# A weight load on another queue, thirteen split-weight buffers and merged small loads in a two-layer decoder

## The chip, the cores and the metric

The kernel runs on one core of one Trainium2 chip. The metric is the device time of one execution in microseconds (us). A core has five engines with queues of their own: TensorE (PE: matmuls; PEld is its weight load), VectorE (DVE), ScalarE (ACT), GpSimd (POOL) and SyncE (SP), which here only issues loads. A load (DMA) is issued from an engine's queue, runs on the core's DMA engines, and tells of its landing by a semaphore.

## The reference

Two decoder layers over 256 tokens of width 1024, in float32:

```python
for i in range(2):
    if i == 0:                                    # gated MLP over 128-position chunks
        u, v, q_mem = split(x @ a_w_in, [768, 1536])
        v = layer_norm(gelu(v), a_ln_v_g, a_ln_v_b)
        mix = gelu(u) * (tril(a_w_s) @ v + a_b_s)  # 12 groups of 64 columns
    else:                                         # causal attention, 12 heads of 64
        q, k, v, q_mem = split(x @ b_w_in, [768, 1536, 2304])
        mix = softmax(mask(q @ k.T / 8)) @ v
    mem_out = cross_attention(q_mem, mem @ w_mem_kv[i])   # 4 heads, 256 memory tokens
    x = layer_norm(ALPHA * x + concat(mix, mem_out) @ w_mix_out[i], ...)
    g, u = split(x @ w_ffn_in[i], 2)              # 2816 columns each
    x = layer_norm(ALPHA * x + (silu(g) * u) @ w_ffn_out[i], ...)
```

## The kernel before

**Split operands.** Matmuls run on float32r operands. To keep float32 accuracy each operand is split into a high part (`split`, L699: ScalarE casts it) and a low part (VectorE subtracts the high part from the original), and each product is three matmuls: high by high, low by high, high by low. So every weight passes through three stations: a load from memory into a `raw` tile, a cast on ScalarE, a subtract on VectorE, into an `spl` tile of which there are `HALF_BUFS` (12). An `spl` tile holds half a weight unit, usually 1024 columns in both parts. The feed-forward layers (`Ffn`, L1019) take their products by a scheme with seven products of sums of blocks (M1 to M7), so VectorE and some loads of GpSimd's queue also add raw weights.

**The planner.** The text of the kernel records every operation in `Plan` (L292), and `simulate` (L389) works out an order for each engine with costs written in the kernel (`Op.cost`, `Wire`). TensorE's operations keep the order of the text. For ScalarE, VectorE, GpSimd and SyncE the planner takes the operation that can start first, with a table `STAGES` (L296) of `(from, slip, idle, margin)` in ns, which says how far it delays a long operation for a short urgent one. Some copies may go to ScalarE or VectorE (`either`, L329), and the planner picks. `free["sync"], free["scalar"]` (L404) say from when on the two engines are taken as free. Then `emit` writes the instructions in that order; waits on semaphores are added for each data dependency. Loads of the SP and ACT queues signal eight completion semaphores (DMAHW0 to DMAHW7) that are given out in turn, in the order in which the instructions are laid out; a load that is given a semaphore which an earlier load still has to signal waits for that landing first.

**The start.** The first product, v = x @ a_w_in (`va` in the profile, L757 to L781), goes over eight row blocks of 128 weight rows. Row block k needs its 128 token rows of the transposed x (tile `x0raw`, here called X0 to X7) and its weight rows (`raw_v`, 768 columns, split into `spl_v`). Those of blocks 0 and 1 are loaded in two halves of 384 columns (192 KB), here W0a, W0b, W1a and W1b; later blocks in one load of 384 KB. For each block TensorE does six matmuls with the first half of the columns and then six with the second: W0a, W0b, W1a, W1b, and so on, in the order of the text. X0 is cast by VectorE, all other tokens and weights by ScalarE. X1 and X2 are issued from ScalarE's queue, behind two small copies (L742) that also make ScalarE load its activation table early; all else from SyncE's. Before all this, 28 matmuls on a constant (`warmup`, L746) keep TensorE busy.

**Small inputs.** The gain and bias of the gate's layer norm (`gv`, L1250) are two loads that repeat a row on 128 partitions; its spatial bias (`bsB`, L1270) six loads of 64 partitions; x for the residual (`xres`, L1329) two loads; the layer-norm gain and bias of layer 1 (`g1mix`, `b1mix`, L1462) two loads of 512 KB into tiles of their own.

Of the kernel before, what the change touches and what calls it, by code (L numbers as in the profile page):

```python
# [13 lines left out]
F32 = mybir.dt.float32  # L14
# [20 lines left out]
RAW_BUFS = 6  # L35
HALF_BUFS = 12
NFF = D_FF // 256
# [254 lines left out]
class Plan:  # L292


    ENGINES = ("tensor", "vector", "scalar", "gpsimd", "sync")
    STAGES = ((0, 300, 700, 300), (360000, 0, 700, 100), (405000, 300, 700, 300))  # L296

# [91 lines left out]
    def simulate(self, stages):  # L389
# [12 lines left out]
        free = {e: 0.0 for e in self.ENGINES}  # L402
        free["sync"], free["scalar"] = 800.0, 2100.0
        busy = dict(free)  # L404
# [280 lines left out]
def build(chip, tc, ins, out):  # L685
    ET = mybir.EngineType
    with (
# [30 lines left out]
        def bcast_row(row, n):  # L718
            return row.rearrange("(o n) -> o n", o=1).to_broadcast([P, n])
# [15 lines left out]
        def const_tile(shape, dtype, name):  # L735
            b = tile_of("const", shape, dtype, name, name)
            b.tile = const.tile(shape, dtype, name=name)
            return b

        mhalf = const_tile([P, 1], F32, "mhalf")  # L740
        chip.vector.memset(mhalf.tile, -0.5)
        for k in (1, 2):  # L742
            nc.scalar.copy(xraw[:, k, :1], mhalf)
        wt = ps.tile([P, 512], F32, tag="mm_3", name="warmup")
# [12 lines left out]
        for i in range(4):  # L757
            raw = raw_tile(f"raw_v{i}")
            for k in range(2):
                kk = 2 * i + k  # L760
                hl = tile_of("spl", [P, 2, 1024], F32R, "spl", f"spl_v{i}_{k}", HALF_BUFS)
                (nc.scalar if kk in (1, 2) else nc.sync).dma_start(xraw[:, kk, :], ins["xT"][kk * P:(kk + 1) * P, :])
                nh = 2 if kk < 2 else 1
                cuts = [(h * W_MIX // nh, (h + 1) * W_MIX // nh) for h in range(nh)]
                rk = raw[:, k * W_MIX:(k + 1) * W_MIX]
                for c0, c1 in cuts:
                    off = OFFS[f"v{i}"][0] + P * (k * W_MIX + c0)
                    nc.sync.dma_start(rk[:, c0:c1], ins["w"][off:off + P * (c1 - c0)].rearrange("(p n) -> p n", p=P))
                if kk == 0:
# [87 lines left out]
        def load_row(t, l, name):  # L857
            nc.sync.dma_start(t, bcast_row(ins[f"ln_{name}"][l, :], D))
            return t

        def load_gb(l, which):
            t = raw_tile(f"gb{l}{which}")
            return [load_row(t[:, i * D:i * D + D], l, f"{which}_{n}") for i, n in enumerate("gb")]


# [383 lines left out]
        gv = raw_tile("gv").rearrange("p (a c) -> p a c", a=2)[:, :, :W_MIX]  # L1249
        nc.sync.dma_start(gv[:, 0, :], bcast_row(ins["a_ln_v_g"][0, :], W_MIX))  # L1250
        nc.sync.dma_start(gv[:, 1, :], bcast_row(ins["a_ln_v_b"][0, :], W_MIX))
        mraws = []
# [16 lines left out]
        for i in range(3):  # L1269
            for j in range(2):  # L1270
                nc.sync.dma_start(bsB[i][j * HD:(j + 1) * HD], ins["bs"][j:j + 1, 2 * i:2 * i + 2, :].to_broadcast([HD, 2, P]))

# [55 lines left out]
        xres = [xr[:, tt, :] for tt in range(2)]  # L1328
        for tt in range(2):  # L1329
            nc.sync.dma_start(xres[tt], ins["x"][tt * P:(tt + 1) * P, :])  # L1330
        gb = load_gb(0, "mix")
# [129 lines left out]
        pts += mem_transposes(pr_mem, "1", (2, 3), acc_tile)  # L1461
        gb = [load_row(tile_of("act", [P, D], F32, t, n), 1, f"mix_{n[0]}") for t, n in (("g1", "g1mix"), ("b1", "b1mix"))]  # L1462
        op = OutProj(1, mix, "c")
# [37 lines left out]
def _pack(inp):  # L1501
# [27 lines left out]
    for i in range(6):  # L1529
# [9 lines left out]
        "wsT": np.ascontiguousarray(inp["a_w_s"][0].transpose(2, 0, 1)),  # L1539
        "bs": np.ascontiguousarray(inp["a_b_s"][0].reshape(6, 2, P).transpose(1, 0, 2)),  # L1540
        "a_ln_v_g": inp["a_ln_v_g"], "a_ln_v_b": inp["a_ln_v_b"],
        "ln_mix_g": inp["ln_mix_g"], "ln_mix_b": inp["ln_mix_b"],
# [21 lines left out]
```

## Time and profile before

| | |
|---|---|
| median of 3 runs | 550.85 us (550.62 to 551.06) |
| the profiled execution's own time | 550.73 us |
| its span, first to last instruction | 549.0 us |
| TensorE busy | 540.2 us (98%) |
| VectorE busy | 505.6 us (92%) |
| ScalarE busy | 358.7 us (65%) |
| loaded and stored | 132.48 MB, 241 GB/s over the span |
| granted TensorE clock, mean | 0.998 |

All times in the profile count from the start of the span. A row of the timeline gives start, length, engine, source line, operation, what it writes and reads, the number of merged instructions, and in brackets the idle time of the engine before it with what ended it. Almost all operations have the line L591, since the planner issues them there; tiles tell them apart. SPq, ACTq and POOLq are instructions that issue loads. Row blocks and halves are left out of the tiles' names: `raw_v` is W0a, W0b and so on, in the order of issue.

### The profile page before, as it was taken

What the parts mean: (1) busy time and instruction counts of PE and PEld (TensorE: products, weight loads), DVE (VectorE), ACT (ScalarE), POOL (GpSimd) and SP (SyncE); (2) the same over time, 40 slices, a digit from 0 to 9 for tenths busy, and PEclk for the clock granted to TensorE, in tenths of its full rate; (3) what the DMA queues carried; (4) which work ended last, traced back from release to release, by engine and by line L of the source; (5) the groups of instructions that cost most, each with busy time, mean ns of one, the idle gap of its engine ahead of it and who ended that gap; (6) DMA issues with size and microseconds to landing.
All of it is one profiled execution on the core that took longest, in us unless ns stands there. A gap on an engine that the chain in (4) does not pass through costs nothing.

```text
span 549.0 us, 7641 instructions
## 1 busy us (share of the span) xinstructions
PE 540.2 (98%) x2858; PEld 459.6 (84%) x2858; DVE 505.6 (92%) x687; ACT 358.7 (65%) x547; POOL 32.7 (6%) x42
## 2 busy tenths in 40 slices
PE   8999999999999999999999999999999999999994
PEld 7988878888888888888898888888888888888884
DVE  5799989999999999998997889889999999999985
ACT  6767845794849585776555689747756684947710
POOL 1110001000001000000000000100000000001001
PEclk9999999999999999999999999999999999999999
DMA  8999963767897979989667222772678979698902
GB/s 294 407 382 393 352 230 109 199 163 243 207 394 182 372 202 292 312 238 386 227 247 290 78 82 82 210 241 78 189 251 236 406 155 422 143 359 224 297 0 77
DMA packets 23637, 132.48 MB, mean 241 GB/s; under 512 B 2608, under 2 KB 6448, under 8 KB 9520
## 3 DMA queue, kind: packets, MB, share of 16 engines
q1 hardware_dynamic: 19856, 109.26, 50.9%
q0 software_dynamic: 3024, 22.02, 21.5%
q10 hardware_dynamic: 720, 0.72, 0.4%
q8 instruction: 22, 0.36, 0.3%
q14 instruction: 15, 0.12, 0.1%
HBM read 120.46 MB, written 1.05 MB: 221 GB/s over the span
## 4 chain that ended last, share of the span: by engine, by line
PE 98%; DMA 1%; DVE 1%; SPq 0%; ACT 0%; issue 0%; DVEq 0%
PE fog L591 11%; PE fof L591 11%; PE Xg L591 10%; PE Xf L591 10%; PE qk L591 6%; PE Zf L591 5%; PE Zg L591 5%; PE opc L591 4%; PE opa L591 4%; PE bv L591 3%; PE pu L591 3%; PE va L591 3%; PE pvm L591 3%; PE Yg L591 2%; PE Yf L591 2%; PE hkm L591 2%
## 5 line engine op out<-in xcount | busy, mean ns | idle before, releaser
L591 DVE TENSOR_TENSOR spl_s_M<-raw_s,spl_s_M 128x1024 fp32r<-128x1024 f32 x140 | 164.9, 1217 | 3.5 <-ACT spl_s_M L591 3.1
L591 ACT CAST spl_s_M<-raw_s 128x1024 fp32r<-128x1024 f32 x140 | 138.7, 1050 | 24.2 <-DMA raw_s<-in_w 19.1
L591 PE MATMUL fof<-spl_w,htf 128*128 128x512 f32 x264 | 63.9, 392 | 0.0
L591 PE MATMUL fog<-spl_w,htg 128*128 128x512 f32 (+1 forms) x282 | 63.9, 378 | 0.0
L591 PEld LDWEIGHTS fog<-spl_w,htg 128*128 128x128 f32 x282 | 50.2, 188 | 9.4
L591 PEld LDWEIGHTS fof<-spl_w,htf 128*128 128x128 f32 x264 | 49.0, 188 | 10.0
L591 DVE TENSOR_TENSOR spl_w<-raw_w,spl_w 128x1024 fp32r<-128x1024 f32 x44 | 53.4, 1216 | 0.0
L591 ACT CAST spl_w<-raw_w 128x1024 fp32r<-128x1024 f32 x44 | 45.6, 1050 | 10.3 <-DMA raw_w<-in_w 10.3
L591 DVE TENSOR_TENSOR raw_s<-raw_s,raw_s 128x2048 f32<-128x2048 f32 x19 | 43.4, 2284 | 0.1
L591 PE MATMUL qk<-x2T,spl_qk 128*128 128x512 f32 x192 | 34.8, 338 | 0.0
L591 PEld LDWEIGHTS qk<-x2T,spl_qk 128*128 128x128 f32 x192 | 29.3, 188 | 4.1
L591 PE MATMUL Zf<-spl_s_M,SfM 128*128 128x512 f32 x120 | 29.0, 390 | 0.0
L591 PE MATMUL Xg<-spl_s_M,SgM 128*128 128x512 f32 x120 | 29.0, 390 | 0.0
L591 PE MATMUL Zg<-spl_s_M,SgM 128*128 128x512 f32 x120 | 28.8, 389 | 0.0
L591 PE MATMUL Xf<-spl_s_M,SfM 128*128 128x512 f32 x120 | 28.8, 389 | 0.0
L591 PE MATMUL Xg<-spl_s_M,x3T 128*128 128x512 f32 x120 | 28.2, 389 | 0.0
L591 PE MATMUL Xf<-spl_s_M,x1T 128*128 128x512 f32 x120 | 28.2, 389 | 0.0
L591 PEld LDWEIGHTS Xg<-spl_s_M,x3T 128*128 128x128 f32 x120 | 22.5, 188 | 4.7
L591 PEld LDWEIGHTS Xf<-spl_s_M,x1T 128*128 128x128 f32 x120 | 22.5, 188 | 4.7
L591 PEld LDWEIGHTS Xf<-spl_s_M,SfM 128*128 128x128 f32 x120 | 22.5, 188 | 4.7
L591 PEld LDWEIGHTS Zg<-spl_s_M,SgM 128*128 128x128 f32 x120 | 22.5, 188 | 4.7
L591 PEld LDWEIGHTS Xg<-spl_s_M,SgM 128*128 128x128 f32 x120 | 22.4, 188 | 4.7
(253 smaller groups left out, 974.9 us busy)
## 6 DMA issues: line engine op xcount, KB each, us to landing
raw_s<-in_w SPq DMA_DIRECT2D x40, 1024.0 KB, 6.8
raw_w<-in_w SPq DMA_DIRECT2D x22, 1024.0 KB, 7.4
raw_s<-in_w POOLq DMA_DIRECT2D x11, 1024.0 KB, 8.5
raw_s<-raw_s POOLq DMA_DIRECT2D x10, 1024.0 KB, 7.6
raw_o<-in_w SPq DMA_DIRECT2D x8, 1024.0 KB, 7.0
raw_qk<-in_w SPq DMA_DIRECT2D x6, 1024.0 KB, 4.8
raw_u<-in_w SPq DMA_DIRECT2D x3, 1024.0 KB, 11.8
raw_bv<-in_w SPq DMA_DIRECT2D x4, 768.0 KB, 7.2
```

The costliest lines, as they stand in the source:

```text
L591: getattr(getattr(self.nc, c.engine), c.name)(*map(real, c.args), **{k: real(v) for k, v in c.kw.items()})
```

## The change

- `HALF_BUFS` goes from 12 to 13. The planner's `STAGES` get other limits at other points, and ScalarE counts as free 250 ns earlier.
- Start: the two small copies that stood ahead of ScalarE's loads go, and one copy of a constant (`one`) stands first on ScalarE. All tokens are issued from SyncE's queue. W0b is issued from ScalarE's queue, and its place in `raw_v` is filled with zeros by GpSimd first, so that the load waits for that fill.
- The gate's gain and bias are one input and one load of 768 KB; the spatial bias is repeated for 64 partitions on the host, and three loads of 128 partitions replace six; x is one load.
- The layer-norm gain and bias of layer 1 lose their own tiles. The class `Halves` loads each in two pieces of 512 columns: the gain into tiles that held the memory queries (`qm`), the bias into two of the nine `work` tiles (both go through `tile_of("act", ...)`).

```diff
-HALF_BUFS = 12
+HALF_BUFS = 13
...
-    STAGES = ((0, 300, 700, 300), (360000, 0, 700, 100), (405000, 300, 700, 300))
+    STAGES = ((0, 150, 700, 100), (135000, 0, 700, 100), (180000, 150, 700, 100))
...
-        free["sync"], free["scalar"] = 800.0, 2100.0
+        free["sync"], free["scalar"] = 800.0, 1850.0
...
+        one = const.tile([P, 1], F32, name="one")
+        chip.scalar.copy(one, chip.const_aps.tensor(1.0, [P, 1], F32))
         mhalf = const_tile([P, 1], F32, "mhalf")
         chip.vector.memset(mhalf.tile, -0.5)
-        for k in (1, 2):
-            nc.scalar.copy(xraw[:, k, :1], mhalf)
...
-                (nc.scalar if kk in (1, 2) else nc.sync).dma_start(xraw[:, kk, :], ins["xT"][kk * P:(kk + 1) * P, :])
+                nc.sync.dma_start(xraw[:, kk, :], ins["xT"][kk * P:(kk + 1) * P, :])
...
-                    nc.sync.dma_start(rk[:, c0:c1], ins["w"][off:off + P * (c1 - c0)].rearrange("(p n) -> p n", p=P))
+                    if kk == 0 and c0:
+                        nc.gpsimd.memset(rk[:, c0:c1], 0.0)
+                    (nc.scalar if kk == 0 and c0 else nc.sync).dma_start(rk[:, c0:c1], ins["w"][off:off + P * (c1 - c0)].rearrange("(p n) -> p n", p=P))
...
+        class Halves:
+
+            def __init__(self, n):
+                self.h = [tile_of("act", [P, 512], F32, f"qm{i}", f"g1mix{i}") if n == "g" else work_tile(f"b1mix{i}")
+                          for i in range(2)]
+                for h, (c0, c1) in zip(self.h, PIECES):
+                    nc.sync.dma_start(h, bcast_row(ins[f"ln_mix_{n}"][1, c0:c1], 512))
+
+            def __getitem__(self, key):
+                return self.h[key[1].start // 512]
...
-        nc.sync.dma_start(gv[:, 0, :], bcast_row(ins["a_ln_v_g"][0, :], W_MIX))
-        nc.sync.dma_start(gv[:, 1, :], bcast_row(ins["a_ln_v_b"][0, :], W_MIX))
+        nc.sync.dma_start(gv, ins["gv"].rearrange("(o a) c -> o a c", o=1).to_broadcast([P, 2, W_MIX]))
...
         for i in range(3):
-            for j in range(2):
-                nc.sync.dma_start(bsB[i][j * HD:(j + 1) * HD], ins["bs"][j:j + 1, 2 * i:2 * i + 2, :].to_broadcast([HD, 2, P]))
+            nc.sync.dma_start(bsB[i], ins["bs"][:, 2 * i:2 * i + 2, :])
...
-        for tt in range(2):
-            nc.sync.dma_start(xres[tt], ins["x"][tt * P:(tt + 1) * P, :])
+        nc.sync.dma_start(xr, ins["x"].rearrange("(a p) d -> p a d", p=P))
...
-        gb = [load_row(tile_of("act", [P, D], F32, t, n), 1, f"mix_{n[0]}") for t, n in (("g1", "g1mix"), ("b1", "b1mix"))]
+        gb = [Halves(n) for n in "gb"]
```

TensorE's instructions stand in the same order in both kernels. What moves at the start stands in two queues. ScalarE's first instructions before (`raw_v0` and `spl_v0_0` are the tiles of W0a and W0b, `spl_v0_1` that of W1a and W1b, `x0raw` the tokens; in brackets the semaphores that an instruction waits for, named by the engine or load that signals them):

```order
L591 ACT_TABLE_LOAD
L591 COPY x0raw_115<-mhalf_75 128x1 [waits DVE_49]
L591 COPY x0raw_115<-mhalf_75 128x1
L591 DMA x0raw_115<-in_xT 128x256 [waits Activation_49] x2
L591 CAST spl_v0_0_131<-raw_v0_113 128x384 [waits DMAHW0_49]
L591 CAST spl_v0_0_131<-raw_v0_113 128x384 [waits DMAHW2_49]
L591 CAST spl_v0_1_149<-raw_v0_113 128x384 [waits DMAHW3_49]
L591 CAST x0T_135<-x0raw_115 128x256 [waits DMAHW4_49]
```

And now:

```order
L741 ACT_TABLE_LOAD
L741 COPY one_75<-const-float32-1.0 128x1
L591 DMA raw_v0_114<-in_w 128x384 [waits DMAHW3_49,Pool_49]
L591 CAST spl_v0_0_131<-raw_v0_114 128x384 [waits DMAHW0_49]
L591 CAST spl_v0_1_141<-raw_v0_114 128x384 [waits DMAHW2_49]
L591 CAST spl_v0_0_131<-raw_v0_114 128x384 [waits DMAHW3_49]
L591 CAST x0T_134<-x0raw_118 128x256
```

Two loads of tokens, which waited for ScalarE's own copies, have become one load, W0b, which waits for GpSimd's fill and for DMAHW3. The cast of W1a now stands ahead of that of W0b.

SyncE's first loads before, W0a, X0, then W0b, W1a and W1b, then those of block 2 and on:

```order
L591 DMA raw_v0_113<-in_w 128x384
L591 DMA x0raw_115<-in_xT 128x256
L591 DMA raw_v0_113<-in_w 128x384 x3
L591 DMA raw_v1_127<-in_w 128x768
L591 DMA raw_v1_127<-in_w 128x768 [waits DMAHW0_49]
L591 DMA x0raw_115<-in_xT 128x256 [waits DMAHW1_49]
```

And now W0a, X0, W1a, X1, W1b, and on:

```order
L591 DMA raw_v0_114<-in_w 128x384
L591 DMA x0raw_118<-in_xT 128x256
L591 DMA raw_v0_114<-in_w 128x384
L591 DMA x0raw_118<-in_xT 128x256
L591 DMA raw_v0_114<-in_w 128x384
L591 DMA raw_v1_127<-in_w 128x768
L591 DMA x0raw_118<-in_xT 128x256
L591 DMA raw_v1_127<-in_w 128x768
L591 DMA x0raw_118<-in_xT 128x256 [waits DMAHW0_49]
L591 DMA raw_v2_137<-in_w 128x768 [waits DMAHW1_49]
L591 DMA x0raw_118<-in_xT 128x256 [waits DMAHW2_49]
L591 DMA raw_v2_137<-in_w 128x768 [waits DMAHW4_49]
```

X1 and X2 have moved in between the weight loads, and W1a has moved up into W0b's place. The ninth, tenth and eleventh load wait for semaphores 0, 1 and 2, the twelfth for 4.

More of the change, by code (lines that the diff above doesn't have):

```diff
@@ L1539, in _pack @@
         "wsT": np.ascontiguousarray(inp["a_w_s"][0].transpose(2, 0, 1)),
-        "bs": np.ascontiguousarray(inp["a_b_s"][0].reshape(6, 2, P).transpose(1, 0, 2)),
-        "a_ln_v_g": inp["a_ln_v_g"], "a_ln_v_b": inp["a_ln_v_b"],
+        "bs": np.repeat(inp["a_b_s"][0].reshape(6, 2, P).transpose(1, 0, 2), HD, axis=0),
+        "gv": np.concatenate([inp["a_ln_v_g"], inp["a_ln_v_b"]]),
         "ln_mix_g": inp["ln_mix_g"], "ln_mix_b": inp["ln_mix_b"],
```

## The prediction

> **What bounds the kernel now.** I read the page first: TensorE is busy for 98% of the span, and the chain that ended last runs 98% on it.
>
> ```profile
> PE 540.2 (98%) x2858; PEld 459.6 (84%) x2858; DVE 505.6 (92%) x687; ACT 358.7 (65%) x547; POOL 32.7 (6%) x42
> PE 98%; DMA 1%; DVE 1%; SPq 0%; ACT 0%; issue 0%; DVEq 0%
> ```
>
> So only a stretch in which TensorE stands still can be won or lost. The waits of TensorE (whom it waited for, us in total, times, longest) name two, and but for the very first instruction there are no others:
>
> ```profile
> PE va L591 <- ACT spl_v L591: 0.8, 1, 0.8
> PE va L591 <- DVE x0T L591: 0.2, 1, 0.2
> ```
>
> Both lie in the first 7 us. The chain in order of time (start, length, what) shows the longer of them, and what follows it:
>
> ```profile
> 1.72 4.33 DMA raw_v<-in_w
> ...
> 6.07 0.52 ACT spl_v L591
> ...
> 6.63 16.01 PE va L591 x90
> ```
>
> W0b, the second half of the first weight rows, is issued at 1.72 and lands at 6.05 (1.72 + 4.33); ScalarE casts it, and TensorE goes on at 6.63. From landing to matmul that is 0.58. In windows (length, TensorE's busy time, clock, DMA share, GB/s) the stretch behind those va matmuls is full to its end at 542.12:
>
> ```profile
> 4.00:6.63 2.63, 1.55 (x6) 1.00 1.01 344
> 22.64:542.12 519.48, 519.47 (x2735) 1.00 0.73 239
> ```
>
> The profiled execution took 550.73 us with a span of 549.0, so 1.7 lies around the span; the median of the runs is 550.85. I sum against 550.73. A measurement of this kernel tells about 0.2% (1.1 us) from no change.
>
> **The start, which sets the time.** The timeline before (start, length, engine, instruction, idle time before it):
>
> ```profile
> 0.84 3.15 PE L746 MATMUL warmup<-const-bfloat16-1.0 128*128 128x128 bf16 x28 [0.84 <-PEq L1553]
> 1.33 0.41 POOL L591 MEMSET mask<- 128x384 f32 x1
> 1.72 2.32 SPq L591 DMA_DIRECT2D raw_v<-in_w  x5
> 2.10 0.28 ACT L591 COPY x0raw<-mhalf 128x1 f32<-128x1 f32 x2
> 2.32 0.86 ACTq L591 DMA_DIRECT2D x0raw<-in_xT  x2
> 3.39 0.51 ACT L591 CAST spl_v<-raw_v 128x384 fp32r<-128x384 f32 x1 [1.01 <-DMA raw_v<-in_w]
> 4.09 0.58 PE L591 MATMUL va<-spl_v,x0T 128*128 128x384 f32 x2
> 4.88 0.97 PE L591 MATMUL va<-spl_v,x0T 128*128 128x384 f32 x4 [0.21 <-DVE x0T L591]
> 6.07 0.33 SPq L591 DMA_DIRECT2D raw_v<-in_w  x1
> 6.07 1.10 ACT L591 CAST spl_v<-raw_v 128x384 fp32r<-128x384 f32 x2 [2.17 <-DMA raw_v<-in_w]
> ```
>
> Three things change here. SyncE's third load becomes W1a in place of W0b, and its fourth becomes X1, the second token rows. W0b goes to ScalarE's queue. And by ScalarE's rows of the new order that load waits for two things: GpSimd (Pool_49), and semaphore DMAHW3. Semaphore 3 belongs to SyncE's fourth load, X1: the first eight loads take 0 to 7, the ninth to eleventh wait for 0, 1 and 2, and the twelfth for 4, because 3 has gone to ScalarE's load. **So W0b can't be issued before X1 has landed**, and ScalarE takes its queue in order: behind that wait stand its first cast, of W0a, and all others.
>
> GpSimd's fill is not what holds it. The fill is as large as the memset of the mask at 1.33, takes that one's place and ends near 1.74 (1.33 + 0.41). ScalarE comes to its load only after one copy, at about 2.2. The mask then moves back 0.4 us, and nobody waits for it there.
>
> When does X1 land? These are single loads of before, the first two the first of SyncE, then those issued at 1.72 and 2.18, then the two of ScalarE at 2.32 and 2.74, then SyncE's at 6.07 (size, us from issue to landing):
>
> ```profile
> raw_v<-in_w SPq DMA_DIRECT2D x1, 192.0 KB, 2.6
> x0raw<-in_xT SPq DMA_DIRECT2D x1, 128.0 KB, 2.4
> ```
>
> ```profile
> raw_v<-in_w SPq DMA_DIRECT2D x1, 192.0 KB, 4.3
> ```
>
> ```profile
> 2.18 0.43 SPq L591 DMA_DIRECT2D raw_v<-in_w  x1
> raw_v<-in_w SPq DMA_DIRECT2D x1, 192.0 KB, 4.5
> x0raw<-in_xT ACTq DMA_DIRECT2D x1, 128.0 KB, 3.9
> ```
>
> ```profile
> x0raw<-in_xT ACTq DMA_DIRECT2D x1, 128.0 KB, 5.0
> ```
>
> ```profile
> raw_v<-in_w SPq DMA_DIRECT2D x1, 384.0 KB, 4.7
> ```
>
> SyncE's fourth load landed at 6.7 (2.18 + 4.5). Now it is 64 KB smaller, and the 128 KB that ScalarE's first load moved meanwhile are gone. At 344 GB/s (the window from 4.00 to 6.63) these 192 KB are 0.6 us, so X1 lands near 6.1; I take 6.05, the landing of the third load of before. Ends: 4.6 (2.18 + 2.4, as fast as the first tokens) and 6.7 (nothing won).
>
> W0b is then issued 0.02 later, as SyncE's load at 6.07 was behind the landing at 6.05. For its landing I take 3.9, ScalarE's first load, which also had its queue to itself beside a busy SyncE: it is 64 KB smaller, but ran in the slow first microseconds. Ends: 2.6 (an empty machine) and 5.0 (ScalarE's second load). So W0b lands at 6.05 + 0.02 + 3.9 = 9.97, and with 0.58 for cast and hand-over TensorE goes on at 10.55 in place of 6.63: **+3.92 us**.
>
> The Trainium skill ("DMA: Bandwidth & Descriptors", section "Issuing engines are not separate DMA queues") speaks against the move: loads of all queues run on the same 16 DMA engines and interleave, and another queue saves issue time alone. By that rule W0b would do no better than SyncE's load issued at 6.07, with its 4.7; the sum would be 0.8 longer, at 555.5. The trace leaves both open, 3.9 and 5.0 being ScalarE's two.
>
> What of this delay lies beside other work? W0a's six matmuls do not hide it: ScalarE issues W0b for some 0.4 (0.86 for two), casts W0a from 6.5 to 7.0, and TensorE has done those six by 8.8 (they took 4.09 to 5.85). It then waits for W0b. The cast of W1a, now ahead of W0b's, is done by 7.6. After 10.55 nothing else is late: a row block costs TensorE 2.1 us (12 of the 90 matmuls in 16.01), and ScalarE and VectorE some 1.3 each (0.84 + 0.40 and 0.96 + 0.42, the cast and subtract of 128x768 and of 128x256), so they catch up; their rows:
>
> ```profile
> L591 ACT CAST spl_v<-raw_v x10: 508/836/839, 3.4 to 14.8; 128x768 fp32r<-128x768 f32 x6, 128x384 fp32r<-128x384 f32 x4
> L591 DVE TENSOR_TENSOR spl_v<-raw_v,spl_v x10: 552/958/960, 3.9 to 15.7; 128x768 fp32r<-128x768 f32 x6, 128x384 fp32r<-128x384 f32 x4
> L591 ACT CAST x0T<-x0raw x7: 396/400/402, 7.1 to 15.5; 128x256 fp32r<-128x256 f32 x7
> L591 DVE TENSOR_TENSOR x0T<-x0raw,x0T x8: 415/418/420, 4.4 to 16.5; 128x256 fp32r<-128x256 f32 x8
> ```
>
> X1 and X2 in SyncE's queue put W1b and block 2's weights back by their issue, 0.4 each (2.32 for five), which the wait for W0b covers. SyncE's later load of u0 now needs semaphore 3 too, so W0b's landing; qm0 is queued ahead of it, and nothing waits.
>
> **The merged and moved loads: nothing.** The gains and biases of the gate were two loads of 384 KB:
>
> ```profile
> L591 DVE SCALAR_TENSOR_TENSOR vn<-vn,mvv,gv x2: 1005/1005/1005, 41.7 to 42.6; 128x768 f32<-128x768 f32 x2
> L591 SPq DMA_DIRECT2D gv<-in_a_ln_v_b x1: 328/328/328, 24.7 to 24.7; - x1
> DMA to landing us min/median/max: 11.1/11.3/11.6
> ```
>
> The later one lands at 36.3 and is first read at 41.7, so 5 us cover the merged one; without cover its price would be the same bytes, 0. The spatial bias and x have more. The layer-norm rows of layer 1 are now loaded in halves amid the attention of that layer, between weight loads, and read first at 363:
>
> ```profile
> L591 DVE SCALAR_TENSOR_TENSOR xres<-xres,mvc,g1mix x4: 741/742/746, 363.0 to 373.6; 128x512 f32<-128x512 f32 x4
> ```
>
> The bias halves hold two of the nine work tiles meanwhile, which softmax uses too.
>
> **Thirteen split buffers and the planner's table** change the order of ScalarE and VectorE; TensorE's own order is the same row by row. Since it never waits after 6.63, they can win 0 there, and lose where the margin is thin. The thinnest place is
>
> ```profile
> 406.58 0.14 PEld L591 LDWEIGHTS tpg<-ident,m5g 128*128 128x128 f32 x1 [0.27 <-DVE m5g L591]
> ```
>
> I take 0 (between -0.3, that wait gone, and +1, a few such waits): VectorE has fewer copies, and 3.9 us more of lead.
>
> Sum: 550.73 + 3.92 = 554.65, so **554.7 us**.
>
> **Rivals.** (1) *The load is not held.* If only the fill held W0b, it would be issued at 2.3 and land at 6.2 (3.9) to 7.3 (5.0); its cast stands behind W1a's (6.05 + 0.52 = 6.6), so TensorE goes on at 7.2 to 7.9: +0.5 to +1.2, say 551.4, not slower by what can be told. For it: at 4.6 + 0.02 + 2.6 + 0.58 = 7.8 even a held load would come to the same, if both it and X1 were as fast as the first loads. Against it: the wait in ScalarE's rows. It decides where X1's landing and W0b's time add up to less than 7.2. Chance 0.12. (2) *Nothing of this waits at all,* and the 0.8 and 0.2 of before go: 549.7. Chance 0.03. (3) *TensorE's clock falls.* At the end TensorE has been idle since 542.1, and the granted clock (the last but two) is whole up to 546.6 and half after:
>
> ```profile
> 542.20:546.60 4.40, 0.00 (x0) 1.00 0.17 56
> 546.70:549.00 2.30, 0.00 (x0) 0.50 0.36 106
> ```
>
> So 4.5 us of idleness halve it. Here TensorE idles from the end of the warm-up matmuls (4.0) to 7.0, and from 8.8 to 10.55: 3.0 and 1.8, less than that. If it is halved all the same, for the 3.1 us that the warm-up needed at the start (0.84 to 3.99), half of that is lost: 1.6, 556.3. The Trainium skill ("TensorE: Matmul & The Clock Gate", "Part 1: The HAM clock gate (the "warmup" mystery)") puts the window at 3.4 us, running free. By that rule a first cast only 0.4 later can meet it in some executions; the row neither shows nor excludes it. Chance 0.13. (4) *The new order stalls the dense part* (work tiles, thin margins), one us on top: 555.7. Chance 0.06.
>
> **How the numbers follow.** The main case has 0.66. Its bounds are 551.9 (4.6 and 2.6) and 556.4 (6.7 and 5.0). The range 552.4 to 556.6 starts half a microsecond above the lower bound, where (1) lies, and ends above the upper one and (3); it leaves out (2), (1) and the far ends. Slower by over 0.2%: 0.66 + 0.13 + 0.06 = 0.85; within: 0.12; faster: 0.03.
>
> **What would show it.** Right: ScalarE's DMA at about 6 in place of 2.3, its first cast at 6.5, the first va matmul near 7.0, a second wait of va for ScalarE up to about 10.5, then 16.0 to the next product and 519.5 to the end of the matmuls as before. Wrong: ScalarE's DMA near 2.3; a cast of W0a at 3.4; a stretch after the start that is longer than before; a clock of 0.5 in the first 20 us.

## The result

The changed kernel took 558.95 us (median of 4 runs, 558.39 to 559.71) beside 550.74 us for the kernel before (4 runs, 550.58 to 551.06): a ratio of 1.0149, 95% interval 1.0137 to 1.0162. It is 8.2 us slower. Forecast were 554.7 us and at most 556.6.

The profiled execution took 558.39 us with a span of 556.5 us; that of before took 550.73 us with a span of 549.0. I compare these two. The page's busy times and the shares of the chain:

```profile
PE 542.4 (97%) x2858; PEld 461.9 (83%) x2858; DVE 500.9 (90%) x678; ACT 362.3 (65%) x555; POOL 32.8 (6%) x43
...
PE 96%; DMA 2%; DVE 1%; SPq 0%; ACT 0%; issue 0%; DVEq 0%; ACTq 0%
```

TensorE is still busy almost throughout. It has the same 2858 matmuls, and two things are new: a wait, and 2.2 us more busy time for the same work. The wait stands in TensorE's waits (whom for, us in total, times, longest):

```profile
PE va L591 <- ACT spl_v L591: 6.2, 2, 3.5
```

The head of the chain (start, length, what) shows what it hangs on:

```profile
2.17 3.44 DMA x0raw<-in_xT
5.61 0.02 issue
5.63 0.02 ACTq L591
5.65 0.04 issue
5.70 6.44 DMA raw_v<-in_w
12.13 0.02 issue
12.15 0.52 ACT spl_v L591
12.67 0.04 issue
12.72 17.42 PE va L591 x90
30.14 5.55 PE hqm L591 x32
```

X1 lands at 5.61, only then does ScalarE issue W0b (5.70), W0b lands 6.44 us later, and TensorE goes on with it at 12.72. Before, that was 6.63: 6.09 us later. Then the same 90 matmuls of `va` take 17.42 us in place of 16.01: another 1.41. Together that is 7.50, and the spans differ by 7.5. The profiled execution was the fastest of the four; the medians' 8.2 have some 0.7 more, which no profile shows. The timeline of the same stretch:

```profile
5.50 0.43 SPq L591 DMA_DIRECT2D x0raw<-in_xT  x1
5.70 0.39 ACTq L591 DMA_DIRECT2D raw_v<-in_w  x1
6.13 0.93 ACT L591 CAST spl_v<-raw_v 128x384 fp32r<-128x384 f32 x2 [3.84 <-DMA x0raw<-in_xT]
...
6.69 2.58 PE L591 MATMUL va<-spl_v,x0T 128*128 128x384 f32 x6 [2.70 <-ACT spl_v L591]
...
12.72 0.69 PE L591 MATMUL va<-spl_v,x0T 128*128 128x384 f32 x1 [3.45 <-ACT spl_v L591]
```

ScalarE's first cast, that of W0a, waits for the landing of X1 and not for W0a, as it stands behind the load in ScalarE's queue. TensorE waits 2.70 before W0a's six matmuls and 3.45 after them.

Where the 1.41 are: windows for the tile `va` alone (length, TensorE's busy time and matmuls, weight loads, ScalarE, clock, DMA share, GB/s):

```profile
12.72:16.00 3.28, 3.28 (x10) 3.28 (x11) 0.00 (x0) 1.00 1.07 406
16.10:30.14 14.04, 14.04 (x81) 13.72 (x79) 0.63 (x2) 1.00 1.03 405
```

Up to 16.0 a matmul takes 0.33 us (3.28 / 10), after it 0.173 (14.04 / 81). TensorE runs at half clock until then. The clock column doesn't tell it: the trace's records of the clock begin only at 16.07 (before, at 3.90), and where there is none the column reads 1.00. The spacing of the matmuls does. All that follows is as long as before (this row counts every engine, VectorE behind the weight loads and GpSimd behind ScalarE):

```profile
30.14:549.43 519.29, 519.28 (x2734) 439.93 (x2733) 484.26 (x645) 347.82 (x530) 29.24 (x31) 1.00 0.72 234
```

519.29 us from the end of `va` to the last matmul, where before had 519.48, and no wait in it.

### The profile page after: what moved, and what is told of

The parts are those of the page before. It is cut to its first block, busy times and chain, and to the rows that moved or that the text cites. A ratio compares the mean times of both kernels' runs of the same rounds, so it can differ in the third digit from the quotient of the medians.

```text
span 556.5 us, 7618 instructions
## 1 busy us (share of the span) xinstructions
PE 542.4 (97%) x2858; PEld 461.9 (83%) x2858; DVE 500.9 (90%) x678; ACT 362.3 (65%) x555; POOL 32.8 (6%) x43
## 4 chain that ended last, share of the span: by engine, by line
PE 96%; DMA 2%; DVE 1%; SPq 0%; ACT 0%; issue 0%; DVEq 0%; ACTq 0%
PE fog L591 11%; PE fof L591 11%; PE Xg L591 10%; PE Xf L591 10%; PE qk L591 6%; PE Zf L591 5%; PE Zg L591 5%; PE opc L591 4%; PE opa L591 4%; PE va L591 3%; PE bv L591 3%; PE pu L591 3%; PE pvm L591 3%; PE Yg L591 2%; PE Yf L591 2%; PE hkm L591 2%
## 5 line engine op out<-in xcount | busy, mean ns | idle before, releaser
L591 PEld LDWEIGHTS Zf<-spl_s_M,SfM 128*128 128x128 f32 x120 | 22.5, 188 | 4.6
```

What stands on the lines that cost most here:

```text
L591: getattr(getattr(self.nc, c.engine), c.name)(*map(real, c.args), **{k: real(v) for k, v in c.kw.items()})
```

## The experiments

Three questions: was it the shared semaphore that held W0b; why did W0b then take 6.44 us and not 3.9; and what halved the clock. Each run has the kernel before beside it on its own chip. Theories A, G and R1 are those that I held after the result; the others are rivals.

### No fill

```diff
-                    if kk == 0 and c0:
-                        nc.gpsimd.memset(rk[:, c0:c1], 0.0)
```

> The changed kernel without the fill: W0b still goes out by ScalarE's queue, but its place is no longer zeroed by GpSimd, and in the new order the load waits for nothing (it is the fourth load laid out and the first to use semaphore 3; X1 gets 4). Theory A (the shared semaphore is the cause: it held W0b for X1's landing and ScalarE's casts behind it): ScalarE's load goes out near 2.2 in place of 5.70, the first cast is back near 3.4, the first va matmul near 4.1, TensorE goes on with W0b between 5.8 and 7.5 in place of 12.72, and the time is 549.9 to 551.7. Rival B (W0b by another queue and the tokens by SyncE's are slow in themselves, held or not): W0b still takes over 6 us and lands at 8.5 or later, TensorE goes on at 9 or later, 553 to 556.

Measured: 552.11 us beside 550.53, ratio 1.0024 (1.0014 to 1.0034). ScalarE's load in the timeline:

```profile
0.87 0.38 ACTq L591 DMA_DIRECT2D raw_v<-in_w  x1
```

And `va` in the chain:

```profile
4.67 19.18 PE va L591 x95
```

The load goes out at 0.87, W0b lands at 3.86, and TensorE doesn't wait for it. Against the kernel before on the same chip 1.6 us are left, so 6.6 of the 8.2 are gone with the fill. What the fill does is put the load later in the order in which semaphores are given out. The time is still 0.4 above the range of theory A: `va` takes 19.2 us, its matmuls 320 ns apart up to 9.7. That is the clock again; TensorE's only wait is 0.7 us between the warm-up and its first matmul.

### The fill by VectorE

```diff
-                        nc.gpsimd.memset(rk[:, c0:c1], 0.0)
+                        nc.vector.memset(rk[:, c0:c1], 0.0)
```

> The changed kernel with the fill of W0b's place kept but done by VectorE instead of GpSimd. In the new order the load then waits for VectorE alone, since it is laid out before X1 and takes semaphore 3 first. Theory A (the semaphore): ScalarE's load goes out near 2.3, as without a fill, TensorE goes on with W0b between 5.8 and 7.5, and the time is 549.9 to 551.9. Rival D (it was the fill, or the wait for it, that cost the time): as the changed kernel, 557 to 560, or between, over 553.

Measured: 552.34 us beside 550.53, ratio 1.0029 (1.0017 to 1.0041). The load:

```profile
1.40 0.39 ACTq L591 DMA_DIRECT2D raw_v<-in_w  x1
```

The fill is still there and waited for, and the load goes out at 1.40. So neither the fill nor the wait for it cost the time: the wait for X1's semaphore did, and rival D is out. As in the run without a fill it is 0.4 above the range, and `va` needs 19.56 us for its 96 matmuls: the clock, which came at 9.88 by the trace's records (without a fill at 9.85).

### Only the start, and all but the start

To the kernel before, only the edits of the start:

```diff
+                    if kk == 0 and c0:
+                        nc.gpsimd.memset(rk[:, c0:c1], 0.0)
-                    nc.sync.dma_start(rk[:, c0:c1], ins["w"][off:off + P * (c1 - c0)].rearrange("(p n) -> p n", p=P))
+                    (nc.scalar if kk == 0 and c0 else nc.sync).dma_start(rk[:, c0:c1], ins["w"][off:off + P * (c1 - c0)].rearrange("(p n) -> p n", p=P))
...
-                (nc.scalar if kk in (1, 2) else nc.sync).dma_start(xraw[:, kk, :], ins["xT"][kk * P:(kk + 1) * P, :])
+                nc.sync.dma_start(xraw[:, kk, :], ins["xT"][kk * P:(kk + 1) * P, :])
```

> The kernel before with nothing but the new start (all tokens by SyncE's queue, W0b by ScalarE's behind GpSimd's fill, the copy of a constant first, ScalarE free from 1850). By its rows the load waits for GpSimd and semaphore 3, X1's, as in the changed kernel. Theory A: the whole loss, 557.5 to 560, with ScalarE's load at about 5.7 and TensorE going on at about 12.7. Rival C (the other edits share in the loss): 554 to 557.

Measured: 558.14 us beside 550.53, ratio 1.0137 (1.0122 to 1.0152). The chain:

```profile
5.53 5.86 DMA raw_v<-in_w
...
11.98 17.73 PE va L591 x90
```

The start alone does nearly all of it, by the same two terms. And the changed kernel with the start of before:

```diff
-                nc.sync.dma_start(xraw[:, kk, :], ins["xT"][kk * P:(kk + 1) * P, :])
+                (nc.scalar if kk in (1, 2) else nc.sync).dma_start(xraw[:, kk, :], ins["xT"][kk * P:(kk + 1) * P, :])
...
-                    if kk == 0 and c0:
-                        nc.gpsimd.memset(rk[:, c0:c1], 0.0)
-                    (nc.scalar if kk == 0 and c0 else nc.sync).dma_start(rk[:, c0:c1], ins["w"][off:off + P * (c1 - c0)].rearrange("(p n) -> p n", p=P))
+                    nc.sync.dma_start(rk[:, c0:c1], ins["w"][off:off + P * (c1 - c0)].rearrange("(p n) -> p n", p=P))
```

> The changed kernel with the start of before (X1 and X2 by ScalarE's queue behind the two small copies, W0b by SyncE's, no fill, ScalarE free from 2100), but with the 13 buffers, the planner's new table, and the merged and halved small loads. Theory A (all of the loss is in the start, the rest costs nothing): 549.9 to 551.3, the same as before within 0.2%; TensorE's only waits are those before 6.7. Rival C (the rest costs something that the late start of the changed kernel hid, as it gave the loads 6 us more lead): 551.8 or more, with a new wait of TensorE after 6.7.

Measured: 551.80 us beside 550.53, ratio 1.0020 (1.0011 to 1.0030), so 0.6 to 1.7 us slower. This lies between A and C, and no wait of TensorE after 6.7 explains it: its waits are 0.5 in all, and its last matmul ends 0.1 later than before (542.22 and 542.12). The rest of this profile's 1.9 us stands behind that (it is the slowest execution of the nine). Its last store, which SyncE issues (us to landing), took

```profile
out<-xres SPq DMA_DIRECT2D x1, 64.0 KB, 3.7
```

against 2.1 in the kernel before and in the changed one. Two runs split these edits.

### The plan alone, the loads alone

The plan (with the halved layer-norm rows, which make room for the 13th buffer), on the kernel before:

```diff
-HALF_BUFS = 12
+HALF_BUFS = 13
...
-    STAGES = ((0, 300, 700, 300), (360000, 0, 700, 100), (405000, 300, 700, 300))
+    STAGES = ((0, 150, 700, 100), (135000, 0, 700, 100), (180000, 150, 700, 100))
...
-        gb = [load_row(tile_of("act", [P, D], F32, t, n), 1, f"mix_{n[0]}") for t, n in (("g1", "g1mix"), ("b1", "b1mix"))]
+        gb = [Halves(n) for n in "gb"]
```

> The kernel before with the 13 split buffers, the planner's new table and the layer-norm rows of layer 1 in halves (without them the 13th buffer doesn't fit); start and other loads as before. It halves the edits of the run that had the start of before and all the rest (551.80, 1.27 above the kernel before). Theory R1 (the cost of the rest lies in the loads; the order of ScalarE and VectorE costs nothing as TensorE never waits): 550.2 to 550.9. Theory R2 (it lies in the new order): 551.3 to 552.3.

Measured: 551.47 us beside 550.77; over the paired rounds the ratio is 1.0008 (0.9999 to 1.0017). And the loads, with the 12 buffers and the table of before:

```diff
-        nc.sync.dma_start(gv[:, 0, :], bcast_row(ins["a_ln_v_g"][0, :], W_MIX))
-        nc.sync.dma_start(gv[:, 1, :], bcast_row(ins["a_ln_v_b"][0, :], W_MIX))
+        nc.sync.dma_start(gv, ins["gv"].rearrange("(o a) c -> o a c", o=1).to_broadcast([P, 2, W_MIX]))
...
-            for j in range(2):
-                nc.sync.dma_start(bsB[i][j * HD:(j + 1) * HD], ins["bs"][j:j + 1, 2 * i:2 * i + 2, :].to_broadcast([HD, 2, P]))
+            nc.sync.dma_start(bsB[i], ins["bs"][:, 2 * i:2 * i + 2, :])
...
-        for tt in range(2):
-            nc.sync.dma_start(xres[tt], ins["x"][tt * P:(tt + 1) * P, :])
+        nc.sync.dma_start(xr, ins["x"].rearrange("(a p) d -> p a d", p=P))
...
-        gb = [load_row(tile_of("act", [P, D], F32, t, n), 1, f"mix_{n[0]}") for t, n in (("g1", "g1mix"), ("b1", "b1mix"))]
+        gb = [Halves(n) for n in "gb"]
```

> The kernel before with the merged loads (gain and bias of the gate, spatial bias, x) and the layer-norm rows in halves, but 12 split buffers, the planner's old table and the start of before: the other half of the rest. Theory R1 (the loads cost it): 551.3 to 552.3. Theory R2 (the new order does): 550.2 to 550.9. One small part of it can be read in the profile: SyncE ends the program by waiting for the eight completion semaphores one after the other, about 0.06 us each, and the number of loads decides which of them the last store signals; that is worth up to 0.2.

Measured: 550.88 us beside 550.77, ratio 0.9999 (0.9991 to 1.0008). The loads cost nothing that can be told (-0.5 to +0.4 us), so R1 is out. For the plan the medians speak for R2 and the paired ratio for 0 to 0.9 us, so whether it costs anything is not shown. The plan's profile again has a late last store (2.9), and its last matmul ends 0.3 later than before. Of the eleven profiles here with the new plan, four have a last store of 2.9 to 3.7; the other seven, that of the changed kernel among them, have 1.9 to 2.4, and the five without the plan 2.1. So the plan doesn't always make the store late; whether it does so more often stays open. The run with 34 warm-up matmuls below has all of these edits too, with the new start, and is -0.3 to +0.9 us from the kernel before.

### The clock kept up

The waits of the changed kernel are left, and TensorE gets work for nobody in them:

```diff
-WARM = 28
+WARM = 56
...
                 for h in range(2):
+                    if kk == 0 and h:
+                        spare = mm_tile("spare")
+                        for n in range(24):
+                            mm(spare[:, :384], xT[:, 0, 0, :P], hl[:, 0, :384], n == 0, n == 23)
```

> The changed kernel with TensorE kept busy through its two waits: 56 warm-up matmuls in place of 28, and between W0a's and W0b's matmuls 24 more products of W0a into a spare tile that nobody reads; the loads and their waits are untouched. Theory A (W0b's landing costs 6.1 us, and a half clock until 16.07 the other 1.4): the clock is full from 7.7 at the latest, W0b still lands at about 12.1, TensorE goes on at about 12.7 and then needs 16.0 for the 90 matmuls, not 17.4; time 556.5 to 557.7, 1.3 to 2.5 below the changed kernel. Rival E (the va matmuls are slow after the wait for another reason, such as operands that come late): they still need 17.4, and the time is 558.4 to 559.8.

Measured: 557.27 us beside 550.77, ratio 1.0113 (1.0099 to 1.0127). The chain:

```profile
8.40 4.17 PE spare L591 x24
12.57 15.60 PE va L591 x90
```

W0b lands at 11.62, 0.5 sooner, but the added matmuls run up to 12.57, so TensorE takes it up only 0.15 sooner; and now the 90 matmuls need 15.60 us, 1.8 less than in the changed kernel. Rival E is out: more work for TensorE made the kernel 1.7 us faster. The idle time itself cost that much, beside the waiting.

### No gap after the warm-up

```diff
-WARM = 28
+WARM = 34
...
-                    if kk == 0 and c0:
-                        nc.gpsimd.memset(rk[:, c0:c1], 0.0)
```

> The changed kernel without the fill, as in the run without the fill above, and with 34 warm-up matmuls in place of 28, so that they end near 4.65, where the first va matmul stood there (4.67), and leave no gap. In that run nothing waited for W0b (it landed at 3.86) and the time was still 552.11, with va matmuls 320 ns apart until the clock was granted at 9.85. Theory A (what was left there is the clock, since 0.7 us of idleness after the warm-up kept it halved): clock full by 4.0 to 6.5 in most executions, TensorE goes on with W0b at 6.3 to 6.7, 550.4 to 551.4. Rival F (the clock does not hang on that gap, or the loss is elsewhere): 551.9 to 552.5 as before.

Measured: 550.94 us beside 550.77, ratio 1.0006 (0.9995 to 1.0016). The chain:

```profile
0.85 3.78 PE warmup L746 x34
4.63 0.11 issue
4.74 17.69 PE va L591 x96
```

Against the run without the fill only six warm-up matmuls are added. They end where the first `va` matmul can start, and `va` takes 17.69 us in place of 19.18: the clock came at 5.45 in place of 9.85. One profile of each could be chance, but without the fill eight of ten executions took over 551.5 us, and with 34 warm-up matmuls one of eleven. So in most executions the gap of 0.7 us between warm-up and work had kept the clock at half. The reverse, on the kernel before:

```diff
-WARM = 28
+WARM = 20
```

> The kernel before with 20 warm-up matmuls in place of 28: they end near 3.1 and leave 1.0 us of idleness before the first va matmul at 4.1; nothing else is changed. Theory A (the clock is granted at the end of a window of 3.4 us that TensorE filled almost whole, so such a gap puts it off): va matmuls 320 ns apart up to between 9 and 13.5, and a median 1 to 2 us above the kernel before. Rival F (the gap plays no part): within 0.3 of it.

Measured: 551.47 us beside 550.57, ratio 1.0018 (1.0009 to 1.0027), so 0.5 to 1.5 us for a warm-up that is 0.9 us shorter. F is out. A's price, 1 to 2, was on the high side: in the profiled execution, one of its fastest, the full clock came at 7.85 and not at 9 or later. Its chain:

```profile
4.03 18.77 PE va L591 x96
```

### The landing of W0b

To see why W0b took 6.44 us I held it by other means, with and without newer loads of SyncE ahead of it. VectorE copies a column of W0a's split into W0b's place, and the load waits for that copy (the gate):

```diff
                 for c0, c1 in cuts:
+                    if kk == 0 and c0:
+                        continue
...
-                    if kk == 0 and c0:
-                        nc.gpsimd.memset(rk[:, c0:c1], 0.0)
...
                 for c0, c1 in cuts:
+                    if kk == 0 and c0:
+                        nc.vector.tensor_copy(rk[:, c0:c0 + 1], hl[:, 1, :1].bitcast(F32))
+                        off = OFFS["v0"][0] + P * c0
+                        nc.scalar.dma_start(rk[:, c0:c1], ins["w"][off:off + P * (c1 - c0)].rearrange("(p n) -> p n", p=P))
                     split(hl[:, 0, c0:c1], hl[:, 1, c0:c1], rk[:, c0:c1])
```

> The changed kernel without GpSimd's fill, but with W0b's load made to wait on purpose for the split of W0a: VectorE copies one column of W0a's low part into W0b's place. By the new order the load then stands on ScalarE's queue behind the casts of W0a, W1a and X1, so it goes out just after X1's landing, at about 6.0, while W0a's casts are no longer behind it. SyncE goes on issuing. Theory G (a load of ScalarE's queue lands behind all that SyncE's queue has issued before it, about 2 MB here): W0b takes 5.8 to 6.5 and lands at 11.8 to 12.5. Rival H (it is a queue of its own and takes the 3.9 of ScalarE's first load in the kernel before): it lands at 9.9. The time by G: TensorE goes on near 12.8, 6.2 later, and the clock has gone to half in the 7 us of idleness before, another 1.7 to 3.4: 558.4 to 560.5; by H 554 to 556.5.

Measured: 560.89 us beside 550.57, ratio 1.0190 (1.0174 to 1.0205). ScalarE issued W0b at 5.67. The DMA view of 5 to 7 us (median us from issue to landing):

```profile
raw_v<-in_w ACTq DMA_DIRECT2D x1, 192.0 KB, 6.5
```

As G said and H did not. The time is above G's range, as TensorE went on only at 14.48: the planner had put W0b's cast behind those of blocks 2 to 5. With the hold added, in `emit` (all of SyncE's loads from the sixth on are kept back until X1 is split; VectorE writes one column of the first one's tile in between):

```diff
+        held, loads, subs, free = [], 0, 0, False
         for op in self.order():
+            if op.engine == "sync" and not free:
+                loads += 1
+                if loads > 5:
+                    held.append(op)
+                    continue
+            put(op)
+            subs += op.name == "tensor_sub" and op.args[1].root.name == "x0raw"
+            if not free and subs == 2:
+                free = True
+                b = held[0].opens[0]
+                b.tile = self.pools[b.pool].tile(b.dims, b.dtype, tag=f"{b.tag}_{b.slot}", name=b.name, bufs=1)
+                self.nc.vector.tensor_copy(b.tile[:, :1], real(op.args[0][:, :1].bitcast(F32)))
+                for o in held:
+                    put(o)
```

> The same, and SyncE's loads of block 2 and later are held back until X1 has been split (VectorE copies one column into the first of them), so that at W0b's issue near 6.0 nothing newer than W1b stands before it. Theory G (order of issue across queues): W0b lands 2.3 to 2.9 after its issue, at 8.3 to 9.0, TensorE goes on with it by 9.6, and the time is 552.5 to 556.5, 3 to 6 below the run with the gate alone though 0.4 us of loads more are late. Rival I (a load by ScalarE's queue at that place takes 6 us whatever SyncE does): it lands at 12 as without the hold, and the time is no shorter, or longer, as block 2 comes later too.

Measured: 563.07 us beside 550.57, ratio 1.0230 (1.0214 to 1.0245). The same view for W0b, issued at 5.63:

```profile
raw_v<-in_w ACTq DMA_DIRECT2D x1, 192.0 KB, 2.4
```

The same load by the same queue at the same time takes 2.4 us in place of 6.5 when SyncE has nothing outstanding but W1b, of which less than 0.01 MB was left to move by then (0.85 MB of SyncE's had moved, all that it had issued). G holds and I is out. But the time went up and not down by 3 to 6: ScalarE, in order, cast blocks 2 to 5 first, and these were later now. Its row in the timeline shows the wait for block 2:

```profile
10.07 0.83 ACT L592 CAST spl_v<-raw_v 128x768 fp32r<-128x768 f32 x1 [3.45 <-DMA raw_v<-in_w]
```

And the chain shows the casts of block 5 and of W0b, and TensorE behind them:

```profile
15.07 1.25 ACT spl_v L592 x2
...
16.36 17.81 PE va L592 x90
```

W0b had been there since 8.01. This left open whether the landing sets the time, so both were run again with one line in the planner's model, which makes it plan W0b's cast right behind the load:

```diff
-        (self.soft if op.engine == "gpsimd" else self.hard).append([op, t + 2350, op.bytes, False])
+        q = self.soft if op.engine == "gpsimd" else self.hard
+        q.insert(0 if op.engine == "scalar" else len(q), [op, t + 2350, op.bytes, False])
```

> The run with the gate alone again, but the planner now takes a load of ScalarE's queue to be served ahead of those of SyncE's (one line in its model of the loads), so that it puts W0b's cast right behind W0b's load and ahead of W1b's and all later ones. SyncE goes on issuing. Theory G: W0b goes out near 5.7, lands near 12.0 behind what SyncE has issued, TensorE goes on with it at about 12.6 in place of 14.48, and the clock has dropped in the 6.7 us of idleness before: 6.0 for the wait and 1.4 to 3.4 for the clock, 558.2 to 560.2. Rival H (with a queue of its own it lands at 9.6): 553.5 to 556.5.

> The run with gate and hold again (SyncE's loads of block 2 and later not before X1 is split), with the same line in the planner's model, so that W0b's cast no longer stands behind those of blocks 2 and 3. Theory G: W0b goes out near 5.65, lands at 8.0 as it did there, TensorE goes on at 8.6 in place of 16.36, block 2 (9.99 there, plus cast and subtract) is needed at 11.75 and ready in time; 2.0 for the wait and 0 to 2.5 for the clock: 552.6 to 555.2, 4 to 7 below the run without the hold. Theory J (the later loads are then late, and TensorE waits for them instead): over 556 with waits of va for block 2 or 3.

Measured: 558.54 us without the hold, ratio 1.0138 (1.0123 to 1.0153), and 554.97 us with it, ratio 1.0073 (1.0057 to 1.0090), beside 550.97. The chain without the hold:

```profile
5.44 6.27 DMA raw_v<-in_w
...
12.30 18.30 PE va L592 x90
```

And with it:

```profile
5.34 2.35 DMA raw_v<-in_w
...
8.28 18.35 PE va L593 x90
```

W0b lands 3.9 us sooner after its issue, TensorE goes on 4.0 us sooner, and the kernel is 3.6 us faster (a little under the 4 to 7 expected), though SyncE's loads are held back for it. J is out: behind the start of `va` TensorE has one wait, and none for a later block:

```profile
PE va L593 <- ACT spl_v L593: 1.8, 1, 1.8
```

### The start without the shared semaphore

To see whether the new start is worth anything by itself, it was put on the kernel before, without the fill and with a warm-up that leaves no gap (tokens by SyncE's queue, W0b by ScalarE's):

```diff
-WARM = 28
+WARM = 34
...
-                (nc.scalar if kk in (1, 2) else nc.sync).dma_start(xraw[:, kk, :], ins["xT"][kk * P:(kk + 1) * P, :])
+                nc.sync.dma_start(xraw[:, kk, :], ins["xT"][kk * P:(kk + 1) * P, :])
...
-                    nc.sync.dma_start(rk[:, c0:c1], ins["w"][off:off + P * (c1 - c0)].rearrange("(p n) -> p n", p=P))
+                    (nc.scalar if kk == 0 and c0 else nc.sync).dma_start(rk[:, c0:c1], ins["w"][off:off + P * (c1 - c0)].rearrange("(p n) -> p n", p=P))
```

> The kernel before with the new start as it may have been meant: all tokens by SyncE's queue, W0b by ScalarE's without any fill or wait, and 34 warm-up matmuls so that no gap is left; 12 buffers, old table, old loads. Theory A: TensorE goes on with W0b at about 6.3 in place of 6.63 and then depends on the landing of block 2; 550.1 to 550.9, so 0 to 0.6 below the kernel before, which the measurement can hardly tell. A rival is that with X1 and X2 ahead of them in SyncE's queue the weights of block 2 land later and give it all back: 550.7 to 551.3.

Measured: 550.75 us beside 550.57, ratio 1.0001 (0.9991 to 1.0010). The chain:

```profile
4.12 5.62 DMA raw_v<-in_w
...
10.44 12.41 PE va L591 x70
```

TensorE takes W0b up at 6.38 in place of 6.63, and gives it back in block 2, where its chain runs over the load of block 3's weights, which lands at 9.74 (4.12 + 5.62). The wait has only moved. No version beat the kernel before.

## Why the prediction was wrong

**The load is held for X1: right.** X1 landed at 5.61 (forecast 6.05, between 4.6 and 6.7) and W0b went out 0.09 later. The two runs that part the load from that semaphore, without a fill and with VectorE's, show that this is the cause: the load then goes out at 0.87 and 1.40. **ScalarE's casts stand behind it: right.** The first cast came at 6.13 (forecast 6.5), the first `va` matmul at 6.69 (7.0).

**W0b's landing in 3.9 us, at most 5.0: this step failed.** It took 6.44 (2.5 more), and this is the larger part of the error. I took ScalarE's first load of before as the like case, since it "had its queue to itself". The queue is not what counts: at 2.32 that load stood behind 704 KB that SyncE had issued (W0a, X0, W0b, W1a) and took 3.9; this one stood behind 1728 KB. Packets of W0b in the changed kernel, by the DMA view of the 3.3 us after its issue (queue 1 is SyncE's, 10 ScalarE's; packets, MB, share of the 16 engines):

```profile
q1 hardware_dynamic: 585, 1.09, 96.8%
```

and of the 3.1 us after that:

```profile
q1 hardware_dynamic: 578, 1.05, 87.8%
q10 hardware_dynamic: 144, 0.20, 17.3%
```

For 3.3 us not one packet of W0b moved, while 585 of SyncE's did; then its 144 went in between SyncE's. In the run with the hold the first of them moved 1.0 us after the issue. W0b landed at 12.13, between SyncE's load issued just before it (11.53) and the one after (12.61). In three other runs (only the start, the clock kept up, the gate alone) it landed 0.2 ahead of a load of SyncE's issued 0.01 to 0.03 before it. So to within that it came in the order of issue over both queues, behind what SyncE had outstanding: W1b, the weights of blocks 2, 3 and 4 (192 + 3 x 384 KB) and X2 to X4 (3 x 128 KB), 1728 KB. With its own 192 KB that is 1.97 MB, at the prediction's 344 GB/s 5.7 us, still 0.7 short. Up to its issue, and from there to its landing, the DMA views have:

```profile
q1 hardware_dynamic: 758, 0.99, 58.9%
```

```profile
DMA packets 1307, 2.35 MB, mean 365 GB/s; under 512 B 145, under 2 KB 777, under 8 KB 1307
```

Of the 2.42 MB that SyncE had issued, about 1.0 had moved, so some 1.4 MB were ahead of W0b. With its own 0.20 and the 2.35 MB that moved meanwhile, some 0.7 MB of SyncE's later loads went in between. What I should have added up is the bytes issued and not yet landed; it comes near, and is no exact sum. The text of the kernel held a hint as well: the planner's model of the loads (`Wire`, L264) puts SyncE's and ScalarE's loads into one list and serves it in order.

The Trainium skill ("DMA: Bandwidth & Descriptors", section "Issuing engines are not separate DMA queues") had it nearer than my sum: loads of all queues interleave on the same engines. By that rule I had given 555.5, with SyncE's load of 4.7 us as the like case, and 4.7 is still 1.7 short. The same page of the Trainium skill, in the section "Queues, rings and completion order", says that each DMA engine takes turns between the queues that have work for it, packet by packet. By that alone W0b's first packets would have come soon after its issue, and the 3.3 us without any don't fit it, unless the load was held in a stage ahead of the DMA engines. Where it waited, no run shows.

**0.58 for cast and hand-over: right**, 0.59 (12.13 to 12.72). TensorE went on at 12.72 and not at 10.55: 2.17 of the error. By luck it isn't more: W0b went out at 5.70, 0.37 ahead of the forecast, and that hid a part of the 2.5.

**16.0 us for the 90 matmuls: wrong**, 17.42, 1.41 of the error. This was rival 3, the halved clock, with a chance of 0.13 and a price of 1.6. The size was right and the chance far too small, and it came on top of the main case where I had made it an alternative. My reason against it was wrong in two ways. I took the 4.5 us of idleness at the end of the kernel before for what it takes to halve a granted clock, and set 3.0 against it. At the end of the changed kernel, idle from 549.4, it took 2.5:

```profile
549.50:551.90 2.40, 0.00 (x0) 1.00 0.00 0
552.00:556.50 4.50, 0.00 (x0) 0.50 0.37 117
```

and in the run with the gate alone, idle from 5.9, it took 1.5 (half from 7.4, below). And I took the clock as granted when the warm-up ends. By the trace's records that is so in some executions only: with 28 warm-up matmuls it was granted at 3.90 in the kernel before, and at 4.51, 5.99 and 6.04 in three more profiles with the start of before (all but the start, the plan, the loads), in which work follows the warm-up within 0.1 us. There that work completed it. In the changed kernel's profile it had not been granted at 4.0, nothing followed for 2.7 us, and it came at 16.07. A granted clock was probably lost, too: two of the four executions of the changed kernel have a mean granted clock of 0.988 in place of 0.996, and the two gate runs without the hold, whose profiles show it granted at 4.0 and half again from 7.4 to 17.6, have 0.986 to 0.990. Gap by gap the runs agree: 0.1 us costs nothing that can be told, 0.7 (no fill) 1.2 to 1.5, no gap (34 matmuls) nothing again, and a shorter warm-up on the kernel before 0.9.

The Trainium skill ("TensorE: Matmul & The Clock Gate", "Part 1: The HAM clock gate (the "warmup" mystery)") gives a free-running window of about 3.4 us that must be busy. The traces agree on its length: by its records the run with the gate alone has the full clock from 3.99 to 7.40, one such window, and then half of it for 10.2 us, three of them, after TensorE fell idle:

```profile
7.40:17.60 10.20, 3.12 (x10) 3.12 (x11) 7.48 (x13) 7.11 (x13) 0.00 (x0) 0.50 0.98 346
```

**The dense part unchanged: right**, 519.29 against 519.48. **Merged loads, 13 buffers, new table at 0 (-0.3 to +1): the loads right, the rest open.** The loads are at 0 (-0.5 to +0.4 by their run). For all of it 0.6 to 1.7 were measured with the start of before, with the middle at the upper bound, but -0.3 to +0.9 with the new start and no gap. Up to the last matmul the profiles of all but the start and of the plan alone are only 0.1 and 0.3 behind; where the rest comes from is not settled.

The sum again: 550.73 + 6.09 + 1.41 = 558.23, and 0.16 are left to the 558.39 of the profile. The run with hold and early cast, in which W0b landed quickly, came out at 554.97, near the 554.7 forecast, but not for the forecast's reason: it had a wait of 1.65 (8.28 less 6.63) and 2.34 for the clock (18.35 less 16.01).

## What to carry to other kernels

Before you move a load to another queue, read in the order of the program which completion semaphore it gets, and whose landing that semaphore still has to tell. Then add up the bytes that the other queue has issued and not yet landed at that moment: here the load came behind them, and their sum gave 5.7 of the 6.4 us. And look at what follows a warm-up: it has to run into real work without a gap, since 0.7 us of idleness there cost 1.2 to 1.5 us here, at half clock.

## What the runs showed of the hardware

- A load of ScalarE's queue landed behind what SyncE's queue had outstanding: 5.9 to 6.5 us from issue to landing in five runs with 1.6 to 1.8 MB issued and not yet landed, 2.35 to 2.38 us in two with a single load of 192 KB not yet landed, whose packets had moved. Its first packet moved 3.4 to 3.8 us after the issue in the one case, 1.0 in the other.
- After 28 warm-up matmuls (3.1 us) a gap of 0.7 us kept TensorE's clock at half until 9.85 in the profiled execution, though it was TensorE's only wait; matmuls of 384 columns were 320 ns apart in place of 173. Two of the ten executions of that run (550.86 and 550.96 us) show no such loss.
- A granted clock went back to half 1.0 to 1.5 us after TensorE fell idle in the three gate runs that had it granted by 4.0, and 2.3 to 5.0 us after the last matmul at the ends of the sixteen profiles.
- More matmuls made a kernel faster: 52 that nobody reads, in the waits of the changed kernel, took 1.7 us off it.
- The landing of the last store (64 KB) took 1.9 to 2.4 us in twelve of the sixteen profiles and 2.9 to 3.7 in four, and the end of the kernel moved with it.
